# Windowed and memory attention on one Trainium2 core with GpSimd's share of the work moved to VectorE and ScalarE

## The chip, the cores and the metric

The kernel runs on one core of a Trainium2 chip. The metric is the device time of one execution in microseconds, the median of several runs. The engines that matter here are TensorE (PE, and PEld for its weight loads), VectorE (DVE), ScalarE (ACT), GpSimd (POOL) and SyncE (SP), which only issues DMAs.

## The reference

The program is two blocks one after the other on a sequence of 1024 tokens of width 1024, in float32. The first block has two layers. Layer 0 mixes with windowed grouped-query attention (16 query heads in 4 groups, head width 64, window 128) and with a memory attention (4 heads of width 128 over 256 memory rows); layer 1 mixes with a recurrence and the same kind of memory attention. Each layer ends in a squared-ReLU MLP. The second block is a gated linear attention with pooling, which the change does not touch. What the change touches is this:

```python
def partial_rotary(t, positions):            # first 16 of 64 dims
    rot = jnp.concatenate([t1 * cos - t2 * sin, t2 * cos + t1 * sin], axis=-1)

def window_gqa(q, k, v, sinks):              # per block of 128 queries, 3 blocks of keys
    scores = einsum(qb, kb) * (ATTN_HEAD_DIM ** -0.5), masked
    m = jnp.maximum(jnp.max(scores, axis=-1, keepdims=True), s)
    p = jnp.exp(scores - m)
    probs = p / (jnp.sum(p, axis=-1, keepdims=True) + jnp.exp(s - m))
    out = einsum(probs, vb)

def memory_attention(mq, mk, mv):
    p = jax.nn.softmax(einsum(mq, mk) * (MEM_HEAD_DIM ** -0.5), axis=-1)
    out = einsum(p, mv)
```

## The kernel before

Every float32 product is made of reduced-precision parts: an operand is split into a high part h and a remainder l, and three matmuls (lines 154 to 156) add h·h, h·l and l·h. A split costs one ScalarE copy (h) and one VectorE subtraction (l). That is why TensorE is busy almost all the time, and why VectorE and ScalarE carry a stream of splits beside it.

The attention layer (attn_layer, L433) runs in stages, each a `weave` of two generators: one gives large products (gemm, L158, "mm" below), the other gives attention. First the memory keys and values are made beside the first projections. Then memory attention (mem_attn, L325, 8 steps of a head and half the tokens) runs beside the key and query projections, each of which ends in the rotary step (rope, L423). Then the windowed attention starts beside the last projections; after that PSUM is handed out anew (L506), and the windowed attention goes on beside two products of the output projection (out_part, L387). The first of these, on the memory heads, needs nothing of the windowed attention. The second, on groups 0 and 1, cannot use group 1's outputs before the last block of group 1 is done. The third, on groups 2 and 3, follows the windowed attention (L514).

The windowed attention is 32 units: 4 groups g times 8 query blocks j, each with 4 heads. win_scores (L571) does for each head two score matmuls into a PSUM tile `sc` (256 or 384 columns), and VectorE adds the mask and takes the maximum into an SBUF tile `wP` (L586). When all four are there, VectorE negates the maxima (`wn`, L590) and prepares `we` (L592), ScalarE takes four exponentials with row sums (L595) and one of `we` (L593), VectorE adds and inverts (L596, L597), and GpSimd multiplies each head's row by its factor (L599). win_values (L602) runs two units later: TensorE transposes the heads into `pt`, ScalarE and VectorE split them (`wPT`, L613, L614), TensorE multiplies with V into `po`. V is stored as [h | l] side by side, so po holds two halves of 64 rows that have to be added: ScalarE copies both to SBUF (L621), GpSimd adds them in four pieces into `ao` (L625). There is one PSUM bank for `po`, three for `sc`, three for `pt`, and one for `mm` while out_part runs beside.

In rope VectorE shuffles (L426), GpSimd multiplies by the sine (L427), VectorE multiplies by the cosine and adds (L428, L429). In mem_attn GpSimd multiplies the exponentials by the inverse sum (L351); mem_attn serves both layers.

The order on each engine is not the code's. The program is built under a scheduler (schedule_with_timeline_sim) which places every instruction by the times that it expects, so an edit of some instructions can change the order of all that stands near them. Each engine takes its instructions in that order.

Of the kernel before, what the change touches and what calls it, by code (L numbers as in the profile page):

```python
# [11 lines left out]
AF = mybir.ActivationFunctionType  # L12
ALU = mybir.AluOpType
# [6 lines left out]
HB = 512  # L20
# [25 lines left out]
class Core:  # L46
# [278 lines left out]
    def mem_attn(self, kv, mq, outs):  # L325

        nc = self.nc
# [3 lines left out]
        def scores(h, half, qh, ql):  # L331
            ks = slice(h * W, (h + 1) * W)
            Ps = self.a("mP")
            for b2 in range(2):
                ps = self.pb("sc")
                for j in range(2):
                    tb = half * 4 + b2 * 2 + j
                    c = slice(tb * P, (tb + 1) * P)
                    self.mm3(ps[:, j * W : (j + 1) * W], qh[:, c], ql[:, c], mkh[:, ks], mkl[:, ks], True, True)
                nm = self.small(2, "mm")  # L340
                p3 = ps.rearrange("p (j m) -> p j m", j=2)
                nc.vector.tensor_reduce(nm, p3, axis=mybir.AxisListType.X, op=ALU.max, negate=True)
                sm = self.small(2, "ms")
                for j in range(2):
                    nc.scalar.activation(Ps[:, (b2 * 2 + j) * W : (b2 * 2 + j + 1) * W], ps[:, j * W : (j + 1) * W],
                                         AF.Exp, bias=nm[:, j : j + 1], accum_out=sm[:, j : j + 1])
                ri = self.small(2, "mr")
                nc.vector.reciprocal(ri, sm)
                for j in range(2):
                    s = slice((b2 * 2 + j) * W, (b2 * 2 + j + 1) * W)  # L350
                    nc.gpsimd.tensor_scalar(Ps[:, s], Ps[:, s], ri[:, j : j + 1], 1.0, op0=ALU.mult, op1=ALU.mult)  # L351
            return Ps

        def values(h, half, Ps, o):
# [19 lines left out]
        for h in range(4):  # L374
            qh, ql = self.split(mq(h), "mq")
            o = self.a("mo")
            for half in range(2):
                Ps = scores(h, half, qh, ql)
# [44 lines left out]
    def rope(self, t, C, S):  # L423
        nc = self.nc
        q = self.b("rsw")
        nc.vector.stream_shuffle(q, t, list(range(8, 16)) + list(range(8)) + list(range(16, 32)))  # L426
        nc.gpsimd.tensor_tensor(q, q, S, op=ALU.mult)  # L427
        nc.vector.tensor_tensor(t, t, C, op=ALU.mult)  # L428
        nc.vector.tensor_tensor(t, t, q, op=ALU.add)  # L429
        return t  # L430
# [140 lines left out]
    def win_scores(self, g, j, Q2, K2):  # L571
        nc = self.nc
        b0, nb = self.win_blocks(j)
        w = nb * P
        m0 = (b0 - j + 1) * P
        ksl = slice(b0 * P, b0 * P + w)
        qsl = slice(j * P, (j + 1) * P)
        mx = self.small(4, "wm")
        sm = self.small(4, "ws")
        Pt = [self.a("wP") for _ in range(2)]  # L580
        pv = [Pt[h // 2][:, (h % 2) * 384 : (h % 2) * 384 + w] for h in range(4)]
        for h in range(4):
            ps = self.pb("sc")
            nc.tensor.matmul(ps[:, :w], Q2[h][:, qsl], K2[0][:, ksl], start=True, stop=False)  # L584
            nc.tensor.matmul(ps[:, :w], Q2[h][:, qsl], K2[1][:, ksl], start=False, stop=True)  # L585
            nc.vector.tensor_tensor_reduce(pv[h], ps[:, :w], self.mask[:, m0 : m0 + w], 1.0,  # L586
                                           self.sinks[:, 4 * g + h : 4 * g + h + 1], op0=ALU.add, op1=ALU.max,
                                           accum_out=mx[:, h : h + 1])
        nm = self.small(4, "wn")
        nc.vector.tensor_scalar(nm, mx, -1.0, None, op0=ALU.mult)  # L590
        es = self.small(4, "we")
        nc.vector.tensor_tensor(es, self.sinks[:, 4 * g : 4 * g + 4], nm, op=ALU.add)  # L592
        nc.scalar.activation(es, es, AF.Exp)  # L593
        for h in range(4):
            nc.scalar.activation(pv[h], pv[h], AF.Exp, bias=nm[:, h : h + 1], accum_out=sm[:, h : h + 1])  # L595
        nc.vector.tensor_tensor(es, es, sm, op=ALU.add)  # L596
        nc.vector.reciprocal(es, es)  # L597
        for h in range(4):
            nc.gpsimd.tensor_scalar(pv[h], pv[h], es[:, h : h + 1], 1.0, op0=ALU.mult, op1=ALU.mult)  # L599
        return Pt  # L600

    def win_values(self, g, j, Pt, V2, ao):  # L602
        nc = self.nc
        b0, nb = self.win_blocks(j)
        qsl = slice(j * P, (j + 1) * P)
        po = self.pb("po")
        for kb in range(nb):
# [8 lines left out]
            v = V2[:, b * P : (b + 1) * P]  # L616
            nc.tensor.matmul(po, v, pT[:, :HB], start=kb == 0, stop=False)  # L617
            nc.tensor.matmul(po, v, pT[:, HB:], start=False, stop=kb == nb - 1)  # L618
        t = [self.misc(HB)[:64, :] for _ in range(2)]
        for i in range(2):  # L620
            nc.scalar.activation(t[i], po[i * 64 : (i + 1) * 64, :], AF.Copy)  # L621
        for o in range(2):
            for i in range(2):
                s = slice((2 * i + o) * P, (2 * i + o + 1) * P)
                nc.gpsimd.tensor_tensor(ao[i][o * 64 : (o + 1) * 64, qsl], t[0][:, s], t[1][:, s], op=ALU.add)  # L625


    def mlp(self, ly, x, ahead):
# [1013 lines left out]
```

## Time and profile before

| | us |
|---|---|
| median of 3 runs | 3340.05 |
| lowest, highest | 3339.60, 3341.76 |
| the profiled execution | 3346.47 |
| span of its instructions | 3344.7 |
| mean granted TensorE clock | 0.988 |

The page's first part gives the busy time of each engine. A view of stretches gives, for a stretch of the span, its length and then the busy time and the count of instructions of PE, PEld, DVE, ACT and POOL, the granted TensorE clock, the DMA share and GB/s. A row of groups gives line, engine, operation, the program's names, shapes and count, then busy us, mean ns of one, the idle time just before them and what ended it. A row of the timeline gives start, duration, engine, line, operation, tiles and count, and in brackets the idle time before it and what ended it. Durations of neighbours on an engine overlap a little: of instructions that stand back to back, the step from start to start is shorter than the duration, and the step is what adds up.

### The profile page before, as it was taken

How to read it: one execution, taken by the hardware profiler on the slowest of the kernel's cores; microseconds unless marked ns; L12 is line 12 of the kernel's file. 1: busy time of each engine (PE TensorE's matmuls, PEld its weight loads, DVE VectorE, ACT ScalarE, POOL GpSimd, SP SyncE). 2: the span in 40 equal slices, each digit the busy share in tenths (PEclk: the TensorE clock that was granted, in tenths of full speed). 3: DMA queues.
4: the chain of work that ended last, by engine and by line, in shares of the span. 5: the costliest groups of instructions: out<-in, count | busy, mean ns of one | idle time of the engine just before them, and what ended most of it. 6: DMA issues, size and time to landing. Idle time of an engine off the chain costs nothing.

```text
span 3344.7 us, 40271 instructions
## 1 busy us (share of the span) xinstructions
PE 3257.2 (97%) x15484; PEld 2711.0 (81%) x15484; DVE 2173.6 (65%) x2716; ACT 1380.9 (41%) x1941; POOL 657.1 (20%) x623
## 2 busy tenths in 40 slices
PE   8998999999999998989999999999999999999998
PEld 6887787888888886777788888888888888887887
DVE  7588777755676669996586568676544454647334
ACT  5335775433443456663444344334422232224121
POOL 0135551232200004431012320000011111212020
PEclk9998999999999999999999999999999999999999
DMA  5355312344776642235324458663412222225532
GB/s 206 131 176 183 83 51 85 131 157 154 272 271 235 231 134 82 86 116 195 108 100 151 159 202 311 230 219 104 167 62 88 70 82 76 76 76 198 186 126 88
DMA packets 155888, 489.94 MB, mean 146 GB/s; under 512 B 17584, under 2 KB 23216, under 8 KB 155696
## 3 DMA queue, kind: packets, MB, share of 16 engines
q1 hardware_dynamic: 155696, 487.38, 42.6%
q8 instruction: 121, 1.98, 0.3%
q14 instruction: 71, 0.58, 0.1%
HBM read 346.80 MB, written 140.51 MB: 146 GB/s over the span
## 4 chain that ended last, share of the span: by engine, by line
PE 78%; DVE 7%; issue 3%; DMA 2%; ACT 1%; POOL 1%; SPq 0%; DVEq 0%; ACTq 0%; POOLq 0%
PE mm L154 23%; PE mm L155 23%; PE mm L156 23%; PE sc L1254 1%; PE pt L611 1%; DVE wl L124 1%; PE mo L155 1%; PE mo L156 1%; PE mo L154 1%; DVE lr L986 1%; PE po L617 1%; PE po L618 1%; DMA ws<-in_w_down 0%; PE sc L584 0%; PE sc L585 0%
## 5 line engine op out<-in xcount | busy, mean ns | idle before, releaser
L154 PE MATMUL mm<-xgh,wh 128*128 128x512 f32 x1888 | 745.5, 395 | 1.1 <-ACT misc L770 0.9
L156 PE MATMUL mm<-xgh,wl 128*128 128x512 f32 x1888 | 742.4, 393 | 0.0
L155 PE MATMUL mm<-xgl,wh 128*128 128x512 f32 x1888 | 741.6, 393 | 0.0
L122 ACT ACTIVATE wh<-ws 128x1024 fp32r<-128x1024 f32 x231 | 243.8, 1056 | 559.1 <-PE mm L155 373.7
L154 PEld LDWEIGHTS mm<-xgh,wh 128*128 128x128 f32 x1888 | 356.4, 189 | 76.4 <-ACT misc L770 1.8
L156 PEld LDWEIGHTS mm<-xgh,wl 128*128 128x128 f32 x1888 | 356.6, 189 | 74.2 <-issue 0.5
L155 PEld LDWEIGHTS mm<-xgl,wh 128*128 128x128 f32 x1888 | 356.6, 189 | 73.4 <-issue 1.2
L124 DVE TENSOR_TENSOR wl<-ws,wh 128x1024 fp32r<-128x1024 f32 x231 | 297.9, 1291 | 100.1 <-ACT wh L122 99.4
L155 PE MATMUL mm<-T,wh 128*128 128x512 f32 x512 | 199.3, 389 | 0.0
L154 PE MATMUL mm<-oh,wh 128*128 128x512 f32 x384 | 152.0, 402 | 3.7 <-DVE mqr L179 2.6
L156 PE MATMUL mm<-oh,wl 128*128 128x512 f32 x384 | 151.4, 394 | 0.0
L155 PE MATMUL mm<-B,wh 128*128 128x512 f32 x384 | 150.0, 391 | 0.0
L745 ACT ACTIVATE wh<-ws 128x512 fp32r<-128x512 f32 x84 | 50.0, 627 | 176.5 <-PE mm L155 91.9
L746 DVE TENSOR_TENSOR wl<-ws,wh 128x512 fp32r<-128x512 f32 x84 | 64.8, 798 | 86.2 <-ACT wh L745 72.7
L677 POOL TENSOR_TENSOR ta<-hm 128x512 f32<-128x512 f32 x28 | 39.8, 1422 | 397.8 <-ACT hm L674 368.6
L155 PEld LDWEIGHTS mm<-T,wh 128*128 128x128 f32 x512 | 96.1, 188 | 20.5 <-DVE T L824 0.4
L975 POOL TENSOR_SCALAR lr<-lr 128x1024 f32<-128x1024 f32 x16 | 27.1, 1693 | 378.6 <-ACT lr L973 377.2
L395 DVE TENSOR_TENSOR xr<-mm,xr 128x512 f32<-128x512 f32 (+1 forms) x80 | 63.5, 794 | 58.2 <-PE mm L156 57.9
L155 PE MATMUL mm<-y,wh 128*128 128x512 f32 x256 | 100.2, 391 | 0.0
L156 PE MATMUL mm<-yh,wl 128*128 128x512 f32 x256 | 100.2, 391 | 0.0
L154 PE MATMUL mm<-yh,wh 128*128 128x512 f32 x256 | 99.3, 393 | 0.0
L1269 POOL TENSOR_TENSOR ge<-G 128x512 f32<-128x512 f32 x24 | 31.1, 1297 | 327.4 <-DMA G<-G 131.4
(533 smaller groups left out, 7722.4 us busy)
## 6 DMA issues: line engine op xcount, KB each, us to landing
ws<-in_w_down SPq DMA_DIRECT2D x144, 512.0 KB, 4.0
ws<-in_w_up SPq DMA_DIRECT2D x64, 512.0 KB, 3.8
T<-h SPq DMA_DIRECT2D x64, 512.0 KB, 5.4
B<-h SPq DMA_DIRECT2D x48, 512.0 KB, 5.5
h<-ta SPq DMA_DIRECT2D x64, 256.0 KB, 2.0
h<-tb SPq DMA_DIRECT2D x64, 256.0 KB, 3.3
h<-hn SPq DMA_DIRECT2D x56, 256.0 KB, 2.4
ws<-in_w_out SPq DMA_DIRECT2D x24, 512.0 KB, 3.6
```

The lines of the kernel that those rows point to most:

```text
L122: nc.scalar.activation(wh, st, AF.Copy)
L124: (lo or nc.vector).tensor_tensor(wl, st, f32(wh), op=ALU.subtract)
L154: mm(ps, wh, xh, start=start, stop=False)
L155: mm(ps, wh, xl, start=False, stop=False)
L156: mm(ps, wl, xh, start=False, stop=stop)
L395: self.gemm((wh[:, c], wl[:, c]), X, lambda o, ps: nc.vector.tensor_tensor(x[m][:, o], ps, x[m][:, o], op=ALU.add))
L611: nc.tensor.transpose(pt[:, h * P : (h + 1) * P], Pt[h // 2][:, c0 : c0 + P], self.ident)
L617: nc.tensor.matmul(po, v, pT[:, :HB], start=kb == 0, stop=False)
L618: nc.tensor.matmul(po, v, pT[:, HB:], start=False, stop=kb == nb - 1)
L677: add(ta[:, lo], hm[:, lo], hm[:, hi], op=ALU.subtract)
L745: act(h[:, n], t[:, n], AF.Copy)
L746: tt(l[:, n], t[:, n], f32(h)[:, n], op=ALU.subtract)
```

## The change

Four places change, and GpSimd has no work left in the attention of layer 0 nor in the memory attention of layer 1. The scaling of the memory softmax goes to VectorE. The sine product of rope goes to VectorE. Of the four heads of a unit the first two are scaled on VectorE, the other two on ScalarE. Of the two halves of po only the upper is copied by ScalarE; VectorE adds the lower out of PSUM to that copy, in four pieces, straight into ao.

```diff
@@ mem_attn
-                    nc.gpsimd.tensor_scalar(Ps[:, s], Ps[:, s], ri[:, j : j + 1], 1.0, op0=ALU.mult, op1=ALU.mult)
+                    nc.vector.tensor_scalar(Ps[:, s], Ps[:, s], ri[:, j : j + 1], None, op0=ALU.mult)
@@ rope
-        nc.gpsimd.tensor_tensor(q, q, S, op=ALU.mult)
+        nc.vector.tensor_tensor(q, q, S, op=ALU.mult)
@@ win_scores
-            nc.gpsimd.tensor_scalar(pv[h], pv[h], es[:, h : h + 1], 1.0, op0=ALU.mult, op1=ALU.mult)
+            if h < 2:
+                nc.vector.tensor_scalar(pv[h], pv[h], es[:, h : h + 1], None, op0=ALU.mult)
+            else:
+                nc.scalar.activation(pv[h], pv[h], AF.Copy, scale=es[:, h : h + 1])
@@ win_values
-        t = [self.misc(HB)[:64, :] for _ in range(2)]
-        for i in range(2):
-            nc.scalar.activation(t[i], po[i * 64 : (i + 1) * 64, :], AF.Copy)
+        t = self.misc(HB)[:64, :]
+        nc.scalar.activation(t, po[64:, :], AF.Copy)
         for o in range(2):
             for i in range(2):
                 s = slice((2 * i + o) * P, (2 * i + o + 1) * P)
-                nc.gpsimd.tensor_tensor(ao[i][o * 64 : (o + 1) * 64, qsl], t[0][:, s], t[1][:, s], op=ALU.add)
+                nc.vector.tensor_tensor(ao[i][o * 64 : (o + 1) * 64, qsl], po[:64, s], t[:, s], op=ALU.add)
```

In the changed file the scalings are L600 (VectorE) and L602 (ScalarE); the later lines are three or two further down: L616 and L617 split the transposes, L620 and L621 multiply with V, L623 copies, L627 adds. The scheduler's order differs in three regions: the attention of layer 0, the memory attention of layer 1, and a handful of places at the start of the second block. The order on TensorE, VectorE and ScalarE moves in the first of them throughout.

TensorE at the end of the last query projection (tile mm_2428 before, mm_2426 now), before the output projection can begin; sc_2121 to 2133 is unit 1, sc_2228 to 2240 unit 2, sc_2364 and on (2362 and on now) unit 3, po_2331 is unit 0. Before:

```order
L154 MATMUL mm_2428<-xgh_143,wh_2398 128x512
L155 MATMUL mm_2428<-xgl_144,wh_2398 128x512
L156 MATMUL mm_2428<-xgh_143,wl_2400 128x512
L617 MATMUL po_2331<-wPT_2337,V_351_1922 128x512
L584 MATMUL sc_2364<-K_349_1916,Q_352_1924 128x384
L585 MATMUL sc_2364<-K_350_1919,Q_352_1924 128x384
```

Now:

```order
L154 MATMUL mm_2426<-xgh_143,wh_2396 128x512
L155 MATMUL mm_2426<-xgl_144,wh_2396 128x512
L156 MATMUL mm_2426<-xgh_143,wl_2398 128x512
L584 MATMUL sc_2129<-K_349_1916,Q_354_1930 128x384
L585 MATMUL sc_2129<-K_350_1919,Q_354_1930 128x384
L584 MATMUL sc_2133<-K_349_1916,Q_355_1933 128x384
L585 MATMUL sc_2133<-K_350_1919,Q_355_1933 128x384
L614 MATMUL pt_2332<-ident,wP_2012 128x128
```

Before, the scores of units 0 to 2 and the transposes of unit 0 stood ahead of the end of the projections; now the scores of half of unit 1 and all of unit 2, and the transposes of unit 0, stand behind it.

VectorE where group 1 ends and the second product of the output projection waits for it; ol_3857 and ol_3861 (ol_3825 and ol_3829 now) are group 1's remainders. Before:

```order
L597 RECIPROCAL we_3786<-we_3786 128x4
L596 TENSOR_TENSOR we_3886<-we_3886,ws_3865 128x4
L597 RECIPROCAL we_3886<-we_3886 128x4
L614 TENSOR_TENSOR wPT_3905<-pt_3900,wPT_3905 128x512
L614 TENSOR_TENSOR wPT_3915<-pt_3910,wPT_3915 128x512
L145 TENSOR_TENSOR ol_3857<-ao_2962,oh_3856 128x1024
L145 TENSOR_TENSOR ol_3861<-ao_2963,oh_3860 128x1024
```

Now:

```order
L600 TENSOR_SCALAR wP_3736<-wP_3736,we_3756 128x384 x2
L627 TENSOR_TENSOR ao_2950<-po_3797,misc_3818 64x128
...
L596 TENSOR_TENSOR we_3854<-we_3854,ws_3833 128x4
L597 RECIPROCAL we_3854<-we_3854 128x4
L600 TENSOR_SCALAR wP_3834<-wP_3834,we_3854 128x384 x2
L617 TENSOR_TENSOR wPT_3873<-pt_3868,wPT_3873 128x512
L617 TENSOR_TENSOR wPT_3883<-pt_3878,wPT_3883 128x512
L145 TENSOR_TENSOR ol_3825<-ao_2950,oh_3824 128x1024
L145 TENSOR_TENSOR ol_3829<-ao_2951,oh_3828 128x1024
```

The scalings and the additions into ao now stand in VectorE's own queue, between the inverse and the splits.

TensorE after the last matmul of the second product of the output projection, where only windowed attention is left (mm_5021 before, mm_4965 now). Before:

```order
L156 MATMUL mm_5021<-oh_3860,wl_4868 128x512
L618 MATMUL po_4933<-wPT_4949,V_866_4116 128x512
L617 MATMUL po_4933<-wPT_4959,V_866_4116 128x512
L611 MATMUL pt_5046<-ident,wP_4792 128x128 x2
L611 MATMUL pt_5046<-ident,wP_4793 128x128 x2
L584 MATMUL sc_5086<-K_864_4110,Q_935_4436 128x256
```

Now:

```order
L156 MATMUL mm_4965<-oh_3828,wl_4814 128x512
L584 MATMUL sc_4920<-K_845_4072,Q_911_4386 128x384
L585 MATMUL sc_4920<-K_846_4075,Q_911_4386 128x384
L584 MATMUL sc_4924<-K_845_4072,Q_912_4389 128x384
L585 MATMUL sc_4924<-K_846_4075,Q_912_4389 128x384
L584 MATMUL sc_4928<-K_845_4072,Q_913_4392 128x384
L585 MATMUL sc_4928<-K_846_4075,Q_913_4392 128x384
L620 MATMUL po_4879<-wPT_4885,V_847_4078 128x512
```

Before, two heads' scores were left behind this point (of the last unit); now eight heads' (all of the last two units).

## Rows read from the trace of the kernel before

**Rows 1.** The page's first part: busy us, share of the span, instructions.

```profile
PE 3257.2 (97%) x15484; PEld 2711.0 (81%) x15484; DVE 2173.6 (65%) x2716; ACT 1380.9 (41%) x1941; POOL 657.1 (20%) x623
```

**Rows 2.** Stretches: length, busy us of PE, PEld, DVE, ACT, POOL, clock, DMA.

```profile
119.00:225.00 106.00, 104.77 (x562) 89.68 (x561) 80.28 (x103) 44.91 (x107) 40.73 (x38) 1.00 0.38 132
225.00:271.00 46.00, 45.34 (x210) 37.41 (x208) 37.77 (x57) 13.55 (x28) 17.05 (x11) 1.00 0.64 198
271.00:301.00 30.00, 19.64 (x80) 14.71 (x80) 25.77 (x50) 17.27 (x37) 15.60 (x17) 0.72 0.71 270
301.00:385.00 84.00, 83.97 (x455) 71.63 (x455) 64.85 (x187) 62.94 (x165) 46.81 (x92) 1.00 0.44 112
385.00:408.00 23.00, 20.55 (x86) 14.09 (x85) 18.72 (x51) 19.23 (x48) 15.07 (x26) 0.85 0.10 26
408.00:492.00 84.00, 83.93 (x452) 71.99 (x451) 63.70 (x188) 59.57 (x155) 43.76 (x87) 1.00 0.24 63
492.00:511.00 19.00, 13.50 (x73) 9.77 (x72) 12.93 (x29) 15.49 (x38) 11.11 (x24) 1.00 0.10 28
1525.00:1625.00 100.00, 99.92 (x503) 84.12 (x502) 55.19 (x82) 38.48 (x83) 16.52 (x26) 1.00 0.33 121
```

**Rows 3.** Timeline of TensorE at the three places without a gemm.

```profile
270.60 0.39 PE L617 MATMUL po<-wPT,V 128*128 128x512 f32 x1
...
280.71 0.69 PE L584 MATMUL sc<-K,Q 128*128 128x384 f32 x1 [6.37 <-DVE wm L586]
...
289.94 0.63 PE L154 MATMUL mm<-oh,wh 128*128 128x512 f32 x1
...
384.32 0.39 PE L617 MATMUL po<-wPT,V 128*128 128x512 f32 x1
...
405.71 0.77 PE L154 MATMUL mm<-oh,wh 128*128 128x512 f32 x1
...
491.69 0.39 PE L618 MATMUL po<-wPT,V 128*128 128x512 f32 x1
...
510.16 0.40 PE L154 MATMUL mm<-oh,wh 128*128 128x512 f32 x1
```

**Rows 4.** Timeline of VectorE and GpSimd where the rotary product runs.

```profile
234.53 3.24 POOL L427 TENSOR_TENSOR rsw<-rsw,ropeS 128x1024 f32<-128x1024 f32 x1 [11.22 <-DVE rsw L426]
...
235.46 3.39 DVE L428 TENSOR_TENSOR pr<-pr,ropeC 128x1024 f32<-128x1024 f32 x1
...
276.62 2.30 DVE L596 TENSOR_TENSOR we<-we,ws 128x4 f32<-128x4 f32 x1
```

**Rows 5.** Groups by form, VectorE, 100 to 530 us: busy us, mean ns, idle.

```profile
L124 DVE TENSOR_TENSOR wl<-ws,wh 128x1024 fp32r<-128x1024 f32 x23 | 32.5, 1414 | 2.8 <-ACT wh L122 2.4
L428 DVE TENSOR_TENSOR pr<-pr,ropeC 128x1024 f32<-128x1024 f32 x10 | 22.8, 2282 | 0.0
...
L596 DVE TENSOR_TENSOR we<-we,ws 128x4 f32<-128x4 f32 x32 | 10.5, 329 | 12.4 <-ACT wP L595 9.9 <-ACT we L593 2.5
...
L597 DVE RECIPROCAL we<-we 128x4 f32<-128x4 f32 x32 | 5.5, 173 | 0.5
```

**Rows 6.** Timeline of VectorE early on: forms near the new ones.

```profile
59.81 0.42 DVE L300 TENSOR_TENSOR misc<-mm,mrs 128x256 f32<-128x256 f32 x1
60.16 0.68 DVE L407 TENSOR_SCALAR angn<-ang 128x1024 f32<-128x1024 f32 x1
60.79 1.23 DVE L124 TENSOR_TENSOR wl<-ws,wh 128x1024 fp32r<-128x1024 f32 x1
```

**Rows 7.** Groups by form on ScalarE, 225 to 511 us.

```profile
L595 ACT ACTIVATE wP<-wP,wn 128x384 f32<-128x384 f32 x96 | 57.9, 607 | 24.7 <-DVE wn L590 24.7
...
L621 ACT ACTIVATE misc<-po 64x512 f32<-64x512 f32 x63 | 37.2, 590 | 16.2 <-PE po L618 15.3
```

**Rows 8.** Timeline of GpSimd: the scalings and additions at the second place.

```profile
397.23 4.13 POOL L599 TENSOR_SCALAR wP<-wP,we 128x256 f32<-128x256 f32 x8 [0.35 <-POOL ao L625]
401.32 1.80 POOL L625 TENSOR_TENSOR ao<-misc,misc 64x128 f32<-64x128 f32 x4
```

## The prediction

> **What bounds the kernel now.** I read the busy times first: TensorE is busy 97% of the span, GpSimd 20% [rows 1], so what a change off TensorE can win is time in which TensorE stands, and that only. Then the stretches of the attention of layer 0 [rows 2]. Look at the column of PE against the length. In 119 to 225 (memory attention and projections) TensorE misses 1.2 us, in 225 to 271 0.7, in the two long stretches of 301 to 385 and 408 to 492 less than 0.1 each. It misses 10.4 in 271 to 301, 2.5 in 385 to 408 and 5.5 in 492 to 511, and in the first two of these the granted clock is 0.72 and 0.85, that is part of the time at the lower of its two levels. VectorE at the same time is at 86%, 81% and 68%: these three places wait for chains through VectorE, ScalarE and GpSimd. They are the places where no large product is ready. The timeline shows their length, from the first instruction after the last gemm matmul to the next gemm matmul [rows 3]: 289.94 - 270.60 = 19.3 us where the projections have ended, 405.71 - 384.32 = 21.4 us where group 1 has to finish (with one half of a gemm within, 6 matmuls), 510.16 - 491.69 = 18.5 us where groups 2 and 3 end: 59.2 us. I call them gaps 1, 2 and 3. What the change does to the time is decided there, and by whether the two long stretches stay full. The memory attention of layer 1 lies under a full TensorE too (99.9 of 100 us, VectorE 55% [rows 2]).
>
> **What GpSimd costs VectorE today.** The sine product on GpSimd takes 3.24 us, and the VectorE multiplication beside it 3.39; a 128x4 addition took 2.30 [rows 4]. The cosine product has a mean of 2.28 us over ten, the weight remainder 1.41 over 23 [rows 5], against 1.23 for a 128x1024 form with nothing on GpSimd [rows 6]. So VectorE gets back 10 x (2.28 - 1.23) = 10.5 us and 23 x (1.41 - 1.23) = 4.1. The 128x4 additions have 0.33, and the nearest form without a second tensor 0.17 [rows 5]: 32 x 0.16 = 5.1. Together 19.7.
>
> The rows show the second instruction waiting for the first to end, not both running slower. The Trainium skill has this as a rule (SBUF - State Buffer, section Who interferes with whom): VectorE and GpSimd share a port pair, the lock is exclusive, and a VectorE instruction with two SBUF inputs blocks against a GpSimd instruction that reads SBUF. By this rule the 19.7 come back whole, as in my sum.
>
> **What the change puts on VectorE.** The sine product: 10 x 1.23 = 12.3 us, less than the 14.6 that the product's and the splits' waits give back, so rope is even to slightly better. A factor on one head: the nearest row is the 128x1024 scalar form, whose successor starts 0.63 us later (60.16 to 60.79 [rows 6]); 384/1024 of it is 0.24, and the 128x256 two-tensor form from PSUM steps 0.35 (59.81 to 60.16). I take 0.30, and 0.23 for 256 columns, bounds 0.24 to 0.45. A piece of 64x128 out of PSUM: half of that 0.35 is 0.18, the whole is the upper bound; I take 0.21. Per unit that is 2 x 0.30 + 4 x 0.21 = 1.44 us, 46 us over 32 units (bounds 38 to 74). The memory scaling in layer 0: 32 x 0.23 = 7.4. VectorE's balance over the attention of layer 0 is 12.3 + 46 + 7.4 - 19.7 = +46 us.
>
> **On ScalarE** a unit loses one copy of 0.59 and gains two scalings; the nearest form is the exponential on the same tile, 0.61 [rows 7]. That is at most +0.63 a unit, 20 us over 32 units, on an engine 66% busy over the six stretches from 225 to 511 [rows 2]. GpSimd loses everything, and with it a latency: eight scalings in a row took 4.13 us and four additions 1.80 at gap 2 [rows 8].
>
> **The full stretches.** VectorE has 64.85 and 63.70 us of work in 84 and 84 [rows 2], 77%. Some 21 of the 32 units lie in them: + 21 x 1.44 - 21 x 0.16 = +27, so 155 of 168, 92%. TensorE's order fills them with transposes, scores and gemm by turns, and the one mm bank has to be emptied by VectorE before the next gemm. With 8% to spare I take 1% lost, 1.7 us; none is the lower bound, 5% (8 us) the upper.
>
> **Up to 271.** VectorE gains and loses about 5 us in 150; TensorE misses 1.9 there. I take -1.
>
> **The gaps, by VectorE's queue.** In the order of each program I add the steps of VectorE's instructions from the evacuation of the last gemm to the instruction that ends the gap (the first remainder ol, or the last split of wPT): before 12.2, 15.2 and 11.2 us, now 18.3, 21.6 and 18.6. The sum grows by 6.1, 6.4 and 7.4 = 19.9. Part is the new instructions; part is work that now stands behind the last gemm instead of ahead of it, as the order shows (12 score matmuls and 8 transposes in gap 1, 12 score matmuls in gap 3). This moved work is not lost on TensorE, since the gemms then end earlier: 455 instructions fill the 84 us of 301 to 385, 0.185 each [rows 2], less for short ones; 3.0 us in gap 1, 2.1 in gap 2, 2.5 in gap 3, 7.6 together. Of the gap's 59.2 us VectorE's steps fill 38.6; the rest, 20.6, are waits, mostly on ScalarE's exponentials and copies. If new VectorE work filled these waits, the gaps would not grow and 7.6 would be won; if all waits stay, the gaps grow by 19.9 and 12.3 are lost. I take the waits on GpSimd out: 2.1 in gap 1 (the addition of 2.30 [rows 4] against 0.17), and in gap 2 the 4.13 + 1.80 = 5.9 [rows 8] against some 2.7 for the same on VectorE and ScalarE, 3.2. The waits on ScalarE I leave, because ScalarE gets two scalings a unit there and its copies queue behind them. So +19.9 - 5.3 - 7.6 = +7.0.
>
> **Sum:** +7.0 + 1.7 - 1.0 = +7.7 us. The profiled execution, 3346.47, would be 3354.2. It lies 6.4 us (0.2%) above the median of 3340.05; the terms are the same on both, so I forecast 3340.05 + 7.7 = 3347.8 us. 0.2%, about what a measurement of this kernel can tell from no change, is 6.7 us: the forecast is just beyond it.
>
> **The rivals.**
> Faster: the chains are set by GpSimd's latency. For it: TensorE's 6.37 us wait in gap 1 is for a VectorE that had just lost 2.30 us behind GpSimd [rows 3, 4], and gap 2 ends behind 5.9 us of GpSimd [rows 8]; a shorter gap 1 also keeps the clock up, and at the upper level the work of 281 to 295 would take about half. Then new work hides in the waits and 7.6 are won, with 2 to 4 us of clock: -10 us, 3330. It decides if VectorE, at its new load, is still waiting a quarter of each gap. Against it: VectorE already fills 86% of 271 to 301.
>
> That GpSimd's locking is all there is would follow from the same rule of the Trainium skill (SBUF - State Buffer, as above): every VectorE stall in the gaps would go and nothing come in its place, which is this rival's time.
>
> Unchanged: the scheduler has placed the work so that gaps only trade; +2 us, 3342. For it: half of the new VectorE steps in the gaps are moved, not new.
>
> Much slower: VectorE becomes the bound. At 92% with one mm bank, three sc banks and one po bank, which is now freed by VectorE and not ScalarE, TensorE waits in the long stretches. With the upper price of 74 us instead of 46 VectorE's work there is 155 + 18 = 173 of 168, and TensorE loses some 5 us to saturation and 5% of 168 to waits, 13; with gaps at their upper end of 12.3 that is +25, 3365. It decides once VectorE's work exceeds TensorE's in a stretch.
>
> The Trainium skill speaks for this one (Perfetto Trace Analysis, section Optimizing Scalar/DVE Operations): when VectorE is saturated, offloading to ScalarE or even GpSimd may pay, and the change does the opposite for most of the work. No run here shows VectorE saturated over a long stretch.
>
> **How the numbers follow.** Forecast (3347.8, own range 3343 to 3355) 0.43; of it six tenths lie above the 0.2% line. Unchanged 0.22. Faster 0.16, of which a fifth within 0.2%. Much slower 0.19. Slower: 0.43 x 0.6 + 0.19 = 0.45. Same: 0.17 + 0.22 + 0.03 = 0.42. Faster: 0.13. The range leaves out half of the faster rival and a third of the much slower one: 3331 to 3362.
>
> **What would show it.** In the profile after: VectorE's rows of L428, L124 and L596 at 1.23, 1.23 and about 0.17 (else the lock is not the cause); the scalings at about 0.38 and the additions at about 0.29 each (else the prices are wrong); the three gaps 23 to 26 us long with 7.6 us more TensorE work in them (shorter than 20 means the faster rival); in the two long stretches TensorE misses 1 to 3 us (over 6 means saturation), waiting for VectorE's L586 or L627. A gap 3 at the lower clock, which was at 1.00 before, would add 2 to 4 us. It is wrong as a whole if the gaps shrink although VectorE's queue in them grew, since then not its length but the latency of one engine set them.

## The result

The changed kernel takes 3362.35 us (median of four, 3359.84 to 3365.46); the kernel before, run beside it, 3340.91. The ratio is 1.0063, 95% interval 1.0051 to 1.0076: slower, by 21 us. The forecast had the side right and the size at a third, +7.7 us; the time lies at the very end of its range, 3331 to 3362. The profiled execution has 3363.02 us and a span of 3361.2.

The page's first part after, with the columns of [rows 1]:

```profile
PE 3264.9 (97%) x15484; PEld 2714.1 (81%) x15484; DVE 2231.9 (66%) x2982; ACT 1393.8 (41%) x1973; POOL 441.6 (13%) x293
```

VectorE has 58 us more over the whole program. Where this falls can be read from stretches of the changed kernel, cut where a gap begins and where the next gemm begins (columns of [rows 2]). The last row is a stretch of layer 1's memory attention:

```profile
119.00:267.79 148.79, 146.52 (x748) 124.03 (x746) 116.04 (x184) 54.95 (x125) 0.00 (x0) 1.00 0.48 159
267.79:293.75 25.96, 16.27 (x51) 9.58 (x50) 22.34 (x62) 18.19 (x45) 0.00 (x0) 0.63 0.82 310
293.75:389.16 95.41, 92.77 (x488) 78.19 (x486) 85.34 (x268) 69.84 (x176) 0.00 (x0) 0.97 0.32 81
389.16:415.30 26.14, 20.91 (x97) 14.45 (x96) 23.05 (x72) 22.51 (x58) 0.00 (x0) 0.92 0.26 64
415.30:500.24 84.94, 84.83 (x439) 71.04 (x438) 74.99 (x240) 60.33 (x155) 0.00 (x0) 0.98 0.24 63
500.24:529.92 29.68, 21.38 (x90) 15.79 (x88) 23.23 (x68) 21.10 (x52) 0.00 (x0) 0.77 0.06 18
...
1539.00:1639.00 100.00, 100.00 (x504) 84.57 (x503) 60.58 (x104) 38.70 (x82) 3.43 (x2) 1.00 0.34 126
```

Gaps 1, 2 and 3 are 26.0, 26.1 and 29.7 us long; they were 19.3, 21.4 and 18.5 [rows 3]. Gap 3 grew most, and its granted clock is 0.77, that is part of the time at the lower of the two levels, where 492 to 511 had 1.00 [rows 2]. In layer 1's memory attention TensorE is full in this stretch, as before. A landmark shows how much of the loss has arisen by the end of layer 0's attention: the first matmul of layer 0's MLP (L154 in these rows), in the timelines of TensorE before and after:

```profile
553.49 0.39 PE L156 MATMUL mm<-oh,wl 128*128 128x512 f32 x1
553.72 0.39 PE L154 MATMUL mm<-xgh,wh 128*128 128x512 f32 x1
```

```profile
573.23 0.39 PE L156 MATMUL mm<-oh,wl 128*128 128x512 f32 x1
573.46 0.39 PE L154 MATMUL mm<-xgh,wh 128*128 128x512 f32 x1
```

It comes 19.7 us later: nearly the whole 21 us arise in the attention of layer 0. (The profiled execution before lost some 4 us between 857 and 880 us, in the MLP, which the other one did not, so the spans differ by 16.5 only.)

**Work and loss.** To compare kernels I count the matmul records of each stretch, and price each at the step from start to start at which such matmuls follow each other at the upper clock level (0.2275 us for 512 columns, as 553.49 to 553.72 above; 0.175, 0.1165 and 0.11 for 384, 256 and 128). That sum is TensorE's *work*; length minus work is what it *lost*, by waiting or by a lower clock. A missing record reads as loss, so a single number is good to about 1 us.

| stretch | before: length, work, lost | after: length, work, lost |
|---|---|---|
| 119 us to gap 1 | 151.6, 148.3, 3.3 | 148.8, 145.3, 3.5 |
| gap 1 | 19.3, 4.8, 14.6 | 26.0, 8.0, 18.0 |
| to gap 2 | 94.4, 90.4, 4.0 | 95.4, 88.9, 6.5 |
| gap 2 | 21.4, 13.1, 8.3 | 26.1, 15.1, 11.0 |
| to gap 3 | 86.0, 83.9, 2.1 | 84.9, 80.8, 4.2 |
| gap 3 | 18.5, 10.7, 7.8 | 29.7, 13.6, 16.1 |

The gaps lose 14.4 us more, gap 3 alone 8.3; the long stretches 4.6 more; ahead of gap 1 nothing changes within the precision of the count. Together that is 19.2 of the 19.7 us.

What is lost has two parts. Length minus the busy column of PE is time in which TensorE stood; busy minus work is time in which it ran, but slower than at the upper level (with some tenths for matmuls whose successor had to wait: the column counts their whole duration, 0.39 us, not the step). The rows of the gaps (those of before stand with the gaps' part of why the prediction was right or wrong) give 9.9, 2.5 and 5.5 us of standing before, and 9.7, 5.2 and 8.3 now: 5.3 more. The other part was 4.6, 5.8 and 2.3 and is 8.3, 5.8 and 7.8: 9.2 more, nearly all of it in gaps 1 and 3, where the granted clock fell (0.68 to 0.63 and 1.00 to 0.77).

The waits of TensorE in gap 3 of the changed kernel, from its timeline (only instructions that waited, and the gemm that ends it):

```profile
506.92 0.39 PE L584 MATMUL sc<-K,Q 128*128 128x256 f32 x1 [1.17 <-DVE wm L586]
509.91 0.50 PE L620 MATMUL po<-wPT,V 128*128 128x512 f32 x1 [2.08 <-DVE ao L627]
513.25 2.79 PE L614 MATMUL pt<-ident,wP 128*128 128x128 f32 x12 [0.21 <-DVE wP L600]
518.58 0.79 PE L620 MATMUL po<-wPT,V 128*128 128x512 f32 x1 [2.53 <-ACT wPT L616]
525.49 0.48 PE L620 MATMUL po<-wPT,V 128*128 128x512 f32 x1 [0.34 <-ACT wPT L616]
528.91 0.47 PE L620 MATMUL po<-wPT,V 128*128 128x512 f32 x1 [1.78 <-DVE ao L627]
529.92 0.39 PE L154 MATMUL mm<-oh,wh 128*128 128x512 f32 x1
```

VectorE and ScalarE release it by turns, and twelve transposes take 2.79 us, 0.23 each, twice the step at the upper level. Three explanations offer themselves. **Load**: VectorE's new instructions make the loss. **Release**: po's one bank is now freed by VectorE (L627), behind whatever stands in its queue. **Placement**: the scheduler has left more windowed attention behind the last gemm, where nothing fills TensorE's waits. The "price" of a piece of work, below, is what its instructions take on their engine. What the lower clock makes by itself has no run of its own.

### The profile page after: what moved, and what is told of

It reads as the page before. It is cut to its first block, busy times and chain, and to the rows that moved or that the text cites. A ratio compares the mean times of both kernels' runs of the same rounds, so it can differ in the third digit from the quotient of the medians.

```text
span 3361.2 us, 40025 instructions
## 1 busy us (share of the span) xinstructions
PE 3264.9 (97%) x15484; PEld 2714.1 (81%) x15484; DVE 2231.9 (66%) x2982; ACT 1393.8 (41%) x1973; POOL 441.6 (13%) x293
## 4 chain that ended last, share of the span: by engine, by line
PE 84%; DVE 8%; issue 3%; ACT 2%; POOL 1%; DMA 1%; SPq 0%; DVEq 0%; ACTq 0%; POOLq 0%
PE mm L154 25%; PE mm L155 25%; PE mm L156 25%; PE sc L1256 1%; DVE wl L124 1%; PE mo L156 1%; PE mo L154 1%; PE mo L155 1%; PE pt L614 1%; DVE lr L988 1%; PE po L620 1%; ACT wP L595 1%; PE po L621 0%; DVE wP L586 0%; DVE lr L976 0%
## 5 line engine op out<-in xcount | busy, mean ns | idle before, releaser
L154 PE MATMUL mm<-xgh,wh 128*128 128x512 f32 x1888 | 746.4, 395 | 1.0 <-ACT misc L772 0.9
L154 PEld LDWEIGHTS mm<-xgh,wh 128*128 128x128 f32 x1888 | 357.0, 189 | 76.8 <-ACT misc L772 1.8
L124 DVE TENSOR_TENSOR wl<-ws,wh 128x1024 fp32r<-128x1024 f32 x231 | 289.5, 1254 | 98.1 <-ACT wh L122 97.7
L154 PE MATMUL mm<-oh,wh 128*128 128x512 f32 x384 | 151.7, 401 | 3.6 <-DVE mqr L179 2.2
L748 DVE TENSOR_TENSOR wl<-ws,wh 128x512 fp32r<-128x512 f32 x84 | 72.8, 894 | 85.3 <-ACT wh L747 71.8
L679 POOL TENSOR_TENSOR ta<-ht 128x512 f32<-128x512 f32 x4 | 11.0, 2750 | 764.2 <-ACT ht L676 764.2
L154 PE MATMUL mm<-yh,wh 128*128 128x512 f32 x256 | 99.4, 393 | 0.0
L854 DVE TENSOR_TENSOR x<-x,mm 128x512 f32<-128x512 f32 x112 | 76.3, 682 | 33.4 <-PE mm L156 33.2
L156 PE MATMUL mm<-T1h,wl 128*128 128x512 f32 x240 | 93.4, 389 | 0.0
```

The lines of the kernel that those rows point to most:

```text
L124: (lo or nc.vector).tensor_tensor(wl, st, f32(wh), op=ALU.subtract)
L154: mm(ps, wh, xh, start=start, stop=False)
L156: mm(ps, wl, xh, start=False, stop=stop)
L748: tt(l[:, n], t[:, n], f32(h)[:, n], op=ALU.subtract)
L854: tt(t, t, ps, op=ALU.subtract if i else ALU.add)
```

## The experiments

All ratios are against runs of the kernel before on the same chip. Work and loss in the gaps are counted as above, each from one profiled execution; gap 2 counts here from the last gemm matmul inside it, so "to gap 2" is longer than in the table above (some 3 us before, 7 in the changed kernel). The last column is the loss in the two long stretches. "Left" in a gap means work that the order puts there.

| kernel | us (beside before) | ratio, interval | gap 1 work/lost | gap 2 | gap 3 | stretches |
|---|---|---|---|---|---|---|
| before | | | 4.8/14.6 | 10.1/7.7 | 10.7/7.8 | 4.6, 2.1 |
| changed | +21.4 | 1.0063 (1.0051-1.0076) | 8.0/18.0 | 9.8/9.1 | 13.6/16.1 | 8.5, 4.2 |
| memory alone | +15.4 | 1.0043 (1.0030-1.0056) | 5.0/14.4 | 10.3/7.6 | 17.1/14.9 | 4.2, 1.9 |
| rope alone | +9.3 | 1.0029 (1.0018-1.0040) | 5.7/14.0 | 13.7/13.5 | 17.3/13.8 | 6.4, 2.0 |
| factors alone | +26.6 | 1.0080 (1.0066-1.0093) | 5.0/14.9 | 14.9/12.9 | 17.3/14.7 | 13.5, 5.9 |
| adds alone | +11.0 | 1.0033 (1.0020-1.0045) | 5.0/16.0 | 13.7/12.5 | 9.7/10.4 | 6.6, 2.9 |
| other weave | +4.9 | 1.0016 (1.0007-1.0024) | 5.0/14.5 | 9.9/8.0 | 13.9/13.1 | 4.1, 2.8 |
| factors back | +11.2 | 1.0039 (1.0026-1.0053) | 8.0/17.0 | 12.4/9.6 | 9.7/9.1 | 8.2, 2.9 |
| adds back | +19.9 | 1.0063 (1.0051-1.0076) | 8.0/17.6 | 8.0/9.3 | 14.2/14.2 | 8.3, 4.8 |
| adds from SBUF | +18.6 | 1.0059 (1.0046-1.0071) | 8.0/17.5 | 11.5/8.4 | 17.1/15.9 | 6.6, 7.1 |
| rope and adds | +3.2 | 1.0013 (1.0004-1.0022) | 5.7/15.1 | 9.1/7.2 | 9.4/10.7 | 8.0, 2.8 |
| rope and memory | +7.7 | 1.0024 (1.0014-1.0034) | 8.0/16.2 | 10.1/7.5 | 17.3/12.5 | 4.0, 1.7 |
| factors, VectorE | +12.2 | 1.0036 (1.0022-1.0049) | 4.8/18.2 | 9.7/8.4 | 12.5/11.1 | 3.6, 2.2 |
| factors, ScalarE | +33.7 | 1.0103 (1.0086-1.0120) | 5.0/13.9 | 20.7/25.5 | 16.6/19.0 | 6.6, 2.8 |

### The four parts alone

Each takes one hunk of the change onto the kernel before. Memory:

```diff
-                    nc.gpsimd.tensor_scalar(Ps[:, s], Ps[:, s], ri[:, j : j + 1], 1.0, op0=ALU.mult, op1=ALU.mult)
+                    nc.vector.tensor_scalar(Ps[:, s], Ps[:, s], ri[:, j : j + 1], None, op0=ALU.mult)
```

> The kernel before with one part of the change alone: the scaling of the memory softmax (L351) on VectorE. Nothing in the windowed attention is edited, yet in the program's order the work left on TensorE behind the last gemm of groups 0 and 1 (gap 3) grows from 34 matmuls of po's shape group (25 on po, 40 transposes, 4 scores) to 34 on po, 56 transposes, 22 scores. Load theory (the loss is VectorE's added work in the windowed attention): no added work there, so 0 us, within 3. Release theory (the loss is that po's bank is freed by VectorE's queue): po is freed by ScalarE as before, 0 us, within 3. Placement theory (the loss is the windowed attention that the scheduler left behind a last gemm, where TensorE waits for chains): gap 3 was 18.5 us with 10.7 of work before and 29.7 with 13.4 after, so with about 17 us of work it lasts 33 to 38, and since the work itself is only moved, the loss is +8 to +14 us.

Rope:

```diff
-        nc.gpsimd.tensor_tensor(q, q, S, op=ALU.mult)
+        nc.vector.tensor_tensor(q, q, S, op=ALU.mult)
```

> The kernel before with the sine product of rope (L427) on VectorE alone. L428 and L124 should be at 1.23 us without the GpSimd product beside them. Load theory: even to slightly better, -3 to 0 us. Release theory: the same. Placement theory: the order leaves 17.3 us of work behind the last gemm in gap 3 (10.6 before) and 13.7 in gap 2 (10.1 before): +8 to +16 us.

Factors, two on VectorE and two on ScalarE:

```diff
-            nc.gpsimd.tensor_scalar(pv[h], pv[h], es[:, h : h + 1], 1.0, op0=ALU.mult, op1=ALU.mult)
+            if h < 2:
+                nc.vector.tensor_scalar(pv[h], pv[h], es[:, h : h + 1], None, op0=ALU.mult)
+            else:
+                nc.scalar.activation(pv[h], pv[h], AF.Copy, scale=es[:, h : h + 1])
```

> The kernel before with the softmax factors of a unit shared by VectorE (two heads) and ScalarE (two heads), the rest as before. Load theory: VectorE gets 0.6 of the 1.44 us a unit, so 0.42 of the +21 us: +7 to +10. Release theory: po is freed by ScalarE as before, 0 to +3. Placement theory: the order leaves 17.3 us in gap 3 (10.6 before) and 14.9 in gap 2 (10.1 before): +10 to +18 us.

Adds out of PSUM (with the copy of the upper half alone, as in the change):

```diff
-                nc.gpsimd.tensor_tensor(ao[i][o * 64 : (o + 1) * 64, qsl], t[0][:, s], t[1][:, s], op=ALU.add)
+                nc.vector.tensor_tensor(ao[i][o * 64 : (o + 1) * 64, qsl], po[:64, s], t[:, s], op=ALU.add)
```

> The kernel before with one part alone: the upper half of po is copied by ScalarE, VectorE adds the lower half out of PSUM in four pieces. VectorE gets 0.84 to 0.92 us a unit. Load theory: 0.6 of the +21 us, +11 to +14. Release theory: +14 to +20, with TensorE's waits on L617/L618's bank released by VectorE's ao in the long stretches and in the gaps. Placement theory: the order leaves 9.7 us of work in gap 3 (10.6 before), 13.7 in gap 2 (10.1 before): -3 to +5 us.

They cost 15.4, 9.3, 26.6 and 11.0 us, 62 together, where all four at once cost 21: the costs of the parts don't add. The memory scaling alone, which touches no instruction of the windowed attention, costs 15 us. Its gap 3 (columns of [rows 2]):

```profile
486.21:518.21 32.00, 23.09 (x113) 17.96 (x112) 21.15 (x56) 24.36 (x62) 19.38 (x38) 0.89 0.05 17
```

It begins 5.5 us earlier than gap 3 of before and has 113 records of TensorE, where 492 to 511 had 73 [rows 2]; 17.1 us of work are left in it, and 14.9 are lost instead of 7.8. Load and release say 0 there; placement's mechanism holds, and its +8 to +14 is just passed. Not all of it is that gap. The landmark of layer 0's MLP comes 9.6 us later than before, and 3.6 us more are lost at the end of layer 1's memory attention, a fourth place where TensorE stands, which the prediction had taken for hidden. Before, then memory alone, with 14.8 us of work in both:

```profile
1620.00:1643.00 23.00, 19.14 (x87) 14.04 (x86) 12.00 (x20) 11.31 (x28) 3.72 (x8) 0.93 0.36 124
```

```profile
1624.40:1651.00 26.60, 19.76 (x86) 14.74 (x85) 14.22 (x28) 12.71 (x29) 0.00 (x0) 0.88 0.39 139
```

The changed kernel loses no more there than before (7.3 us against 8.2); why this one does was not tried. Rope alone loses 13.8 in its gap 3. In gap 2 those three kernels that leave 13.7 or more lose 12.5 to 13.5, memory and before 7.6 and 7.7. The totals don't choose cleanly. The adds were too dear for placement's +5 (gap 2 was priced too low), fit load's +11 and stay under release's +14. The factors passed placement's +18 by 8.6 us, most of it lost in the long stretches, where placement had named nothing. Load fails on memory and rope, and prices the factors at less than half.

Rope alone shows what the lock cost. The groups of VectorE by form, 100 to 530 us (columns of [rows 5]):

```profile
L124 DVE TENSOR_TENSOR wl<-ws,wh 128x1024 fp32r<-128x1024 f32 x22 | 27.5, 1252 | 3.3 <-ACT wh L122 3.1
L428 DVE TENSOR_TENSOR pr<-pr,ropeC 128x1024 f32<-128x1024 f32 x10 | 12.2, 1220 | 0.0
...
L596 DVE TENSOR_TENSOR we<-we,ws 128x4 f32<-128x4 f32 x32 | 6.0, 188 | 11.2 <-ACT wP L595 9.2 <-ACT we L593 2.0
```

All three had been longer [rows 5], and come down although GpSimd still scales and adds. VectorE got its time back, and the kernel became slower.

### The same work, placed otherwise

The kernel before, with every operation on its engine as it was and one number of the weave changed:

```diff
-            weave(self.out_part(I["w_out0"][0], outs[:4], xr), 8, win, 26)
+            weave(self.out_part(I["w_out0"][0], outs[:4], xr), 8, win, 22)
```

> The kernel before with all its work on the engines where it was; only one number of the last weave (L513) is 22 instead of 26, which moves nothing in groups 0 and 1 and changes which windowed units stand ahead of the last gemm of the output projection's second product. In the program's order 13.9 us of TensorE work stand behind that gemm (28 on po, 47 transposes, 16 scores), as in the changed kernel (13.5; 28, 44, 16), instead of 10.6 (25, 40, 4). Load theory (loss from VectorE's and ScalarE's added work): 0 us, within 2. Placement theory (the loss of gap 3 comes from what is left behind the gemm, at the prices of before too): gap 3 lasts 27 to 30 us, TensorE loses 13 to 16 in it against 7.8, +5 to +8 us in all.

Its gap 3:

```profile
488.11:515.11 27.00, 20.15 (x92) 14.44 (x91) 18.86 (x44) 19.96 (x45) 16.46 (x32) 0.87 0.07 20
```

It is 27.0 us long and 13.1 are lost, the lower ends of what was forecast; the other columns differ by 0.7 us at most, and the kernel is 4.9 us slower (load had said 0, placement +5 to +8). This is the one run in which placement alone changes. At 13.9 us of work against 13.6 in the changed kernel's gap 3, it makes 5.3 of the 8.3 us there. The clock fell here as well, to 0.87, with every price as before: of the 5.3 us some 1.4 are standing and 4.0 slower running. How much of a gap's length the clock makes by itself was not tried; at the upper level TensorE might have stood instead.

### Parts of the change undone

Factors back on GpSimd:

> The changed kernel with the factors (L600, L602) back on GpSimd; memory scaling, rotary product and the adds out of PSUM stay on VectorE. Load theory: VectorE's added work falls from 1.44 to 0.84 us a unit, the loss from +21 to +12: about 3352. Release theory (po's bank freed by VectorE): nothing changes for po, the loss stays at +15 to +21. Placement theory: the order leaves 9.7 us behind gap 3's gemm instead of 13.5, so gap 3 gives back 6 us, gap 1 stays as in the changed kernel (8.0 us of work left, 18 lost): 3350 to 3356. The two long stretches tell load from placement: load wants them to lose about 6 together instead of 13.

Adds back on GpSimd, both halves copied by ScalarE:

> The changed kernel with po copied by ScalarE in both halves and added by GpSimd as before; memory scaling, rotary product and factors stay on VectorE and ScalarE. Load theory: VectorE has 0.6 us a unit more than before instead of 1.44, the loss falls to +9: about 3349. Release theory: po is freed by ScalarE again, the loss falls to 0 to +7. Placement theory: 14.2 us left behind gap 3's gemm, 8.0 behind gap 1's, as in the changed kernel: 3356 to 3366, near the kernel with the factors alone (3366.7). ScalarE has the two scalings and both copies of a unit, the most of all kernels; if that engine's queue sets the gaps this is the slowest.

Adds on VectorE, but from two copies in SBUF:

```diff
-        t = self.misc(HB)[:64, :]
-        nc.scalar.activation(t, po[64:, :], AF.Copy)
+        t = [self.misc(HB)[:64, :] for _ in range(2)]
+        for i in range(2):
+            nc.scalar.activation(t[i], po[i * 64 : (i + 1) * 64, :], AF.Copy)
...
-                nc.vector.tensor_tensor(ao[i][o * 64 : (o + 1) * 64, qsl], po[:64, s], t[:, s], op=ALU.add)
+                nc.vector.tensor_tensor(ao[i][o * 64 : (o + 1) * 64, qsl], t[0][:, s], t[1][:, s], op=ALU.add)
```

> The changed kernel with po copied by ScalarE in both halves, so that ScalarE frees its bank, and the four adds of a unit on VectorE from the copies in SBUF. VectorE has as many adds as the changed kernel, ScalarE one copy of 0.59 us more a unit. Release theory: TensorE's waits for po behind VectorE's adds (6.0 us in five waits in the changed kernel) go, 3350 to 3357. Load theory: the same VectorE work, 3360 to 3366. Placement theory: 16.7 us left behind gap 3's gemm (13.5 in the changed kernel), 8.0 in gap 1: 3360 to 3368.

Without the factors 10 us come back, and gap 3, with 9.7 us left in it, loses 9.1: both load and placement had said so; the stretches still lose 11.1 together, where load wanted 6. Without the adds nothing measurable comes back, 19.9 of 21.4, where load wanted 9 and release 0 to 7. So release does not carry the loss. The third says the same, though it has 3.5 us more work left in gap 3, which at the ratios of the table could hide a gain of 2 to 4 us. TensorE's waits, 100 to 560 us (total, times, longest), changed kernel and then adds from SBUF:

```profile
PE po L620 <- ACT wPT L616: 7.4, 7, 3.0
PE sc L584 <- DVE wm L586: 6.3, 7, 1.9
PE po L620 <- DVE ao L627: 6.0, 5, 2.1
```

```profile
PE po L620 <- ACT wPT L616: 9.5, 7, 3.6
PE sc L584 <- DVE wm L586: 6.1, 6, 3.0
PE po L621 <- DVE wPT L617: 3.6, 6, 1.2
...
PE po L620 <- ACT misc L624: 1.3, 1, 1.3
```

L617 had 0.4 in the changed kernel. The 6.0 us behind VectorE's adds are gone, and some 6.6 us stand in other rows (2.1 more behind L616, 3.2 more behind L617, 1.3 behind the copy). The engine named last in those waits was not what set the time: it was replaced, and the kernel is at +18.6 against +21.4, with intervals that overlap.

### Two parts together

Rope and adds:

> The kernel before with two parts of the change: the sine product of rope on VectorE, and po's halves added out of PSUM on VectorE (memory scaling and factors stay on GpSimd). In the program's order 5.7 us of TensorE work are left in gap 1, 9.1 in gap 2, 9.7 in gap 3, about as before (5.0, 10.1, 10.6), although each of the two parts alone leaves 13.7 in gap 2 and rope alone 17.3 in gap 3. If the two parts' costs add: +9.3 + 11.0 = +20 us. Load theory: VectorE has 0.84 of the 1.44 us a unit, rope is even or better: +11 to +14. Placement theory: the gaps lose 14 to 16, 8 to 10 and 9 to 10.4 us, as gaps with that much work did in the runs so far, and the stretches 3, 6.5 and 2.9 as with the adds alone: 43.5 to 48 against 41.8, +2 to +6 us, 3343 to 3347.

Rope and memory:

> The kernel before with the two parts of the change that touch nothing of the windowed attention: rope's sine product and the memory scaling on VectorE. Left in the gaps by the order: 8.0, 10.1 and 17.3 us of work. If the two parts' costs add: +15 + 9 = +24 us. Load theory: the windowed attention's prices and engines are those of before, the GpSimd product no longer stops VectorE: -3 to 0 us. Placement theory: gap 1 loses 17 to 18, gap 2 7.6 to 8.5, gap 3 14 to 15.5, and 9 to 12 elsewhere: 48 to 54 against 41.8, +6 to +12 us.

Their orders had been read before they ran, and of the three placement alone gave both totals: +3.2 us, where the two parts cost 9.3 and 11.0 alone, and +7.7 where they cost 9.3 and 15.4. By gap it was less exact: rope and memory lost 16.2 and 12.5 us in gaps 1 and 3, where 17 to 18 and 14 to 15.5 had been said. Gap 3 of rope and adds:

```profile
496.45:516.56 20.11, 13.77 (x64) 11.33 (x63) 15.36 (x43) 12.84 (x31) 4.13 (x8) 0.79 0.09 27
```

64 records, 20.1 us. The kernel has every add of the change on VectorE, and its gap 3 is 9.6 us shorter than the changed kernel's. No run here is faster than the kernel before.

### The factors on one engine

All four on VectorE:

```diff
-            nc.gpsimd.tensor_scalar(pv[h], pv[h], es[:, h : h + 1], 1.0, op0=ALU.mult, op1=ALU.mult)
+            nc.vector.tensor_scalar(pv[h], pv[h], es[:, h : h + 1], None, op0=ALU.mult)
```

> The kernel before with one edit: all four factors of a unit on VectorE instead of GpSimd, nothing on ScalarE. At the step measured in the changed kernel (0.35 to 0.41 us a head) VectorE gets 1.4 to 1.6 us a unit more, as much as by the whole change (1.44 forecast). In the program's order 5.0, 9.7 and 12.5 us of TensorE work are left in the three gaps (before 5.0, 10.1, 10.6; factors shared with ScalarE alone 5.0, 14.9, 17.3). Load theory (VectorE's added work sets the loss): +17 to +21 us. Placement theory: gaps lose 14 to 16, 8 to 9.5 and 12 to 14 us, other stretches some 12 to 14 against 11.7: 46 to 53.5 against 41.8, +4 to +12 us. If ScalarE's two scalings a unit, and not where the work was placed, made the shared factors cost 26.6 us, this kernel is at 0 to +5.

All four on ScalarE:

```diff
-            nc.gpsimd.tensor_scalar(pv[h], pv[h], es[:, h : h + 1], 1.0, op0=ALU.mult, op1=ALU.mult)
+            nc.scalar.activation(pv[h], pv[h], AF.Copy, scale=es[:, h : h + 1])
```

> The kernel before with one edit: all four factors of a unit on ScalarE instead of GpSimd (0.61 us for 384 columns, 0.50 for 256, so some 2.3 us a unit, less nothing). With the four on VectorE the kernel cost 12.2 us and TensorE lost 3.6 and 2.2 us in the two long stretches; with two on each engine it cost 26.6 and lost 13.5 and 5.9. Work left by the order: 5.0, 20.7 and 16.6 us in the gaps. If ScalarE's queue is what the shared factors cost in the stretches, this kernel loses 15 to 25 us in the two stretches together and, with gap 2 at 14 to 18 and gap 3 at 14 to 16, is +30 to +45 us. If the stretches lost through where the work stood and not through ScalarE, they lose 6 to 10 together, the gaps the same, and it is at +16 to +24. VectorE's load cannot matter here: it gets nothing.

On VectorE: gap 1 and the two long stretches.

```profile
272.40:295.33 22.93, 9.26 (x31) 5.83 (x30) 20.24 (x43) 12.54 (x28) 5.84 (x5) 0.65 0.76 284
295.33:392.54 97.21, 96.60 (x517) 82.72 (x516) 89.53 (x254) 68.95 (x177) 23.75 (x49) 0.98 0.43 115
410.61:495.63 85.02, 85.02 (x450) 72.34 (x448) 78.96 (x230) 60.98 (x157) 19.98 (x44) 0.99 0.24 63
```

VectorE is at 92% and 93% of the two stretches, as the prediction had it for the change, and TensorE misses 0.6 and 0.0 us: that load costs nothing here where TensorE has a gemm beside it. In gap 1 it does: VectorE has 20.2 us there against 17.0 before, at the same TensorE work, and 3.6 us more are lost, all by standing (13.7 us against 9.9). The total of +12.2 is at the upper edge of placement's forecast, but the 18.2 us lost in gap 1 are more than the 14 to 16 that it had there. Had ScalarE's two scalings alone made the 26.6 us of the shared factors, the kernel would be at 0 to +5.

On ScalarE: gaps 2 and 3.

```profile
376.87:423.09 46.22, 33.39 (x140) 23.32 (x138) 25.92 (x84) 43.40 (x113) 10.83 (x24) 0.78 0.23 57
503.64:539.20 35.56, 25.35 (x109) 19.08 (x108) 20.66 (x53) 33.49 (x77) 9.54 (x23) 0.81 0.05 15
```

ScalarE is busy 94% of both, gap 2 is 46 us long, and TensorE loses 25.5 and 19.0 us there. The total is that of the forecast by ScalarE's queue, the place is not: the stretches lose 9.4 together, and the gaps more than either forecast allowed. These two gaps cost more for each us of work left in them than in most runs, and ScalarE is the fullest engine in both; that ScalarE's queue makes the difference is argued, not shown.

## Why the prediction was right or wrong

**The locks: right.** By form, 100 to 530 us of the changed kernel; L596 answers to the 329 ns of [rows 5]:

```profile
L124 DVE TENSOR_TENSOR wl<-ws,wh 128x1024 fp32r<-128x1024 f32 x22 | 26.8, 1220 | 2.7 <-ACT wh L122 2.5
L428 DVE TENSOR_TENSOR pr<-pr,ropeC 128x1024 f32<-128x1024 f32 x10 | 12.2, 1220 | 0.0
L427 DVE TENSOR_TENSOR rsw<-rsw,ropeS 128x1024 f32<-128x1024 f32 x10 | 12.2, 1218 | 0.0
...
L596 DVE TENSOR_TENSOR we<-we,ws 128x4 f32<-128x4 f32 x32 | 5.1, 159 | 7.5 <-ACT wP L595 5.6 <-ACT we L593 1.7
```

L428, L124 and L596 were forecast at 1.23, 1.23 and 0.17 us, and have 1.22, 1.22 and 0.16. It agrees with the Trainium skill (SBUF — State Buffer, section Who interferes with whom), as the prediction used it. That this would show in the time was not claimed, and it doesn't: rope alone got it all and lost 9 us.

**The prices: right, the scalings a little dear.** Same view, then ScalarE, 225 to 530 us:

```profile
L627 DVE TENSOR_TENSOR ao<-po,misc 64x128 f32<-64x128 f32 x124 | 29.6, 276 | 2.6 <-ACT misc L623 2.0
L600 DVE TENSOR_SCALAR wP<-wP,we 128x384 f32<-128x384 f32 x48 | 17.9, 416 | 0.3
L600 DVE TENSOR_SCALAR wP<-wP,we 128x256 f32<-128x256 f32 x16 | 4.9, 349 | 0.2
```

```profile
L602 ACT ACTIVATE wP<-wP,we 128x384 f32<-128x384 f32 x48 | 26.7, 608 | 2.9 <-DVE we L597 2.2 <-DVE wn L590 0.6
```

The additions, VectorE's and ScalarE's scalings of 384 columns have 0.28, 0.42 and 0.61 us against 0.29, 0.38 and 0.61. Busy time over count gives some 1.7 us of VectorE a unit (an estimate), where the sum had 1.44.

**Up to gap 1: nothing came.** -1 was forecast. 3.0 us of work have moved from ahead of gap 1 into it, and the gap begins 2.8 us earlier: the loss ahead of it is 3.3 and 3.5 us, the same within the count.

**The long stretches: mis-sized.** 1.7 forecast, 4.6 counted. VectorE is at 89% and 88%, under the 92% forecast. TensorE's busy column misses 2.6 and 0.1 us, inside the 1 to 3 named; before it missed 0.5 and 0.1. The rest of what is lost there, lower clock (0.97 and 0.98; before 0.97 and 0.99) and missing records, is not taken apart. The reason given, VectorE near its limit, is not borne out: at 92 and 93% with all factors on VectorE no more was lost than before. What the stretches lose (5.7 to 19.4 us over the kernels) follows no single price and stays open.

**The gaps: the step that failed.** Forecast +7.0 us, counted +14.4: the sum credited waits on GpSimd that did not come back, and had no term for the clock. It had three terms. The moved work, 7.6 us credited, was right: 8.1 us more TensorE work stand in the gaps. VectorE's queue, +19.9, was right too. The three gaps before, columns of [rows 2]:

```profile
270.61:289.94 19.33, 9.44 (x32) 5.91 (x30) 17.02 (x34) 11.21 (x27) 12.62 (x13) 0.68 0.54 189
384.32:405.71 21.39, 18.94 (x83) 12.79 (x82) 17.11 (x47) 17.67 (x44) 12.78 (x23) 0.88 0.10 31
491.69:510.16 18.47, 12.97 (x70) 9.33 (x69) 13.24 (x29) 15.23 (x37) 10.32 (x23) 1.00 0.10 29
```

VectorE's busy time in them, 47.4 us, became 22.3, 23.1 and 23.2, together 68.6: +21.2. The third term, 5.3 us for the waits on GpSimd, didn't come back: the gaps are 22.6 us longer, as much as VectorE's queue and a little more, and VectorE's idle time in them is 13.2 us, where it was 11.8. The waits in gap 3 above are on L586, L616 and L627, so the likely reading is that GpSimd's latency had been one of several steps of a chain around TensorE, VectorE and ScalarE, and that others took its place; no run tried this. By gap the forecast lengths were 23.3, 24.6 and 25.9, the measured 26.0, 26.1 and 29.7; the worst is gap 3, whose clock stayed up before and fell to 0.77, which the prediction named as a possible 2 to 4 us and left out of the sum. Its first premise, that time in which TensorE stands is all that a change off TensorE can win, leaves this out: of the 14.4 us some 5 are standing and 9 slower running. Whether the gaps would have been shorter at the upper level stays open.

The prediction also saw that work had moved behind the last gemms; it gave TensorE's part back whole, as gemms that end earlier, and put VectorE's part into the queue's +19.9. That isn't all: without any new instruction 3.2 us more work left in gap 3 made it 8.5 us longer (other weave). At like work left, runs without the change's prices in the windowed attention lose 16.2 in gap 1 (rope and memory) and 13.1 in gap 3, the changed kernel 18.0 and 16.1, before 14.6 and 7.8. Of the 11.7 us which these two gaps lose more, about 7 can so be put to the placement and 5 to the new prices; this is an estimate, since the two were never parted in one kernel.

**The rivals.** Much slower came nearest in size (3365), and with the wrong mechanism: neither saturation of VectorE nor po's release by it holds. The range reaches to 3362 only because it takes in most of this rival, so that the measured time just meets it is luck. Faster falls. That GpSimd's work would trade for nothing, Unchanged, is what rope and adds together nearly do, at +3.2 us.

## What to carry to other kernels

Where a scheduler orders the program by its own expectation of times, an edit is two changes: its prices, and where the rest is put. The second can be read from the order before anything runs: count the work that stands behind each place where the filling work runs out. Such a gap, measured once, gives a rough price for that gap: here some 0.7 to 1.2 us lost for each us of work left in gaps 2 and 3, but 2 to 4 in gap 1. So parts of a change must be tried together as well as apart; their costs here were 62 us apart and 21 together. And a gap's granted clock is to be read beside its waits: of what the gaps lost more here, the larger part was slower running, not standing.

An engine at 92 and 93% cost nothing here while the bound engine had independent work beside it; where that had run out, in gap 1, some 3 us more of its instructions cost 3.6 us.

## What was not expected

One number of a weave, with every instruction the same, moved the kernel by 4.9 us. The scaling of the memory softmax cost 15 us, half of it in a gap that begins some 265 us after the last of layer 0's scalings. And with factors on ScalarE alone, an engine at 43% of the whole span was at 94% for two stretches of 46 and 36 us.
